# Four layers on one core: S5's direct term folded into its kernels, kernels made in four column strips, z in three matmuls per block, and steps moved by one head

## The chip, the cores and the metric

The kernel runs on one core of a Trainium2 chip. The core has TensorE (PE), whose weight loads are listed apart (PEld), VectorE (DVE), ScalarE (ACT), GpSimd (POOL) and SyncE (SP), which here only issues DMAs. The metric is the time of the whole program on the device, in microseconds (us), as the median of several runs; lower is better. The profiled execution is one run of its own, and its trace starts with the first and ends with the last instruction (the span).

## The reference

A stack of four mixers, each with a residual and a layer norm, on 256 tokens of width 2048 in float32. The first is an SSD mixer (a state space layer in chunks of 128), the second Fox (attention of 16 heads with a forget gate), the third MLA (latent attention), the fourth S5. The change touches S5 above all:

```python
def s5_mixer(h, w_in, lam_re, lam_im, log_step, b_re, b_im, c_re, c_im, d_skip, w_glu, b_glu, w_out):
    u, z = jnp.split(h @ w_in, 2, axis=-1)
    lam = lax.complex(lam_re, lam_im)
    step = jnp.exp(log_step)[:, None]
    lam_bar = jnp.exp(lam * step)
    b_bar = ((lam_bar - 1.0) / lam)[..., None] * lax.complex(b_re, b_im)
    ug = u.reshape(bsz, T, S5_GROUPS, S5_GROUP).astype(jnp.complex64)
    bu = jnp.einsum('gpi,btgi->btgp', b_bar, ug)
    ...
    _, states = lax.associative_scan(_diag_linear_combine, (a_seq, bu), axis=1)
    y = jnp.einsum('gip,btgp->btgi', c, states).real.reshape(bsz, T, S5_WIDTH) + d_skip * u
    y = jax.nn.gelu(y)
    y = y * jax.nn.sigmoid(y @ w_glu + b_glu)
    y = y * jax.nn.silu(z)
    return y @ w_out
```

S5 has 128 groups of 16 channels with 64 complex states each. The term `d_skip * u` is the direct term (D). In the SSD mixer, what the change moves is the product of the scores `cb` with the decay.

## The kernel before

Every large product is written in three passes for accuracy: a float32 operand is split into a rounded part (hi) and a rest (lo), and hi·hi, hi·lo and lo·hi are summed. A weight block of half a megabyte (128x1024) comes in by DMA as `raw`, ACT writes `whi` (line 119), DVE writes `wlo` (line 120), and PE uses both. `mm3` does three matmuls 256 columns wide. `proj_T` (lines 136 to 157) has another form: one 512-wide matmul of whi with hi and lo side by side (line 147), one 256-wide matmul of wlo with hi (line 148), two halves in PSUM, and a DVE reduction (line 157) that adds the halves.

The order of the work is written out by hand. `C.tick()` is called after each half block of a projection (16 or 24 matmuls); `C.defer(n, f)` puts f behind the n-th tick from now, `C.behind(f)` behind the last matmul written. Engines run their own instructions in the order in which the program has them, and wait for each other's data and buffers.

The stages in the trace: SSD to about 712 us, Fox to about 1240, MLA to about 1583, S5 from there to the end.

In SSD, for each group of heads `scores` (line 560 on) multiplies the decay table `arena` by `cbp`, two DVE instructions (line 567); line 569 defers it by three ticks.

S5's kernels do not depend on the tokens. They are made ahead, by the generator `s5_params` (line 947), most of it in the Fox stage: 16 steps on POOL (lines 1093 to 1145), each for 8 groups, with a store of `pn` (`P_d`) as the last instruction. Behind a step stands its `turn` on PE (from line 1062): four transposes to `wp` (1070), and eight small matmuls `kp` (1077) of `pn` with the block pair `bd`. ACT copies `wp`, DVE copies `kp` to `kt` (1079), and DMAs store both (`W_d`, `K_d`). A step's turn is written when the next step is called. Fox calls one step behind each of the three last strips of its v projection (line 699) and one at the start of each head (line 715).

In S5 the width is cut in four strips ft of 512. `u_strip` projects u (three matmuls), transposes it by chunks of four tokens and forms the chunk inputs `vp` (line 1300). A scan over the 64 chunks runs on DVE in three pieces (lines 1207 to 1213), `SCAN_US` = 1.9 us of it per tick, and beside it PE projects z in 16 blocks (`z_tile`, line 1333, by `proj_T`). Then, per strip: `near` (line 1396) applies the kernels within a chunk, `far` (1412) the kernels from the scanned states with `mats` loaded from `P_d`, DVE adds both (`ys`, 1416), `back1` transposes (yp2, 1425), `back2` transposes again (yp3, 1435) and adds D times u on DVE (`yt`, 1441), and `gelu` follows a tick later. A list `held` with the function `outputs` sets after how many ticks a strip's half is taken up. After z comes the glu projection, which needs the gelu's results strip by strip, and the output projection.

## Time and profile before

| | us |
|---|---|
| median of 3 runs | 2019.85 (2015.91 to 2023.44) |
| the profiled execution | 2021.63 |
| its span | 2019.8 |
| mean granted TensorE clock | 0.991 |

The page gives busy time per engine first, then the chain of work that ended last, followed back from the last instruction, and the groups of instructions by line. The prediction below quotes the rows on which it rests. A group's row reads: line, engine, operation, result<-operands with their shapes, count, busy time and mean in ns, then the idle time of the engine ahead of it and what ended most of it. A row of the windows view reads: the stretch and its length, for each engine the busy time and the number of instructions (in the order PE, PEld, DVE, ACT, POOL), the granted clock, the DMA share and GB/s. A row of the timeline reads: start, duration, engine, line, operation and count, and in brackets the idle time before and what ended it.

### The profile page before, as it was taken

The numbers are of one execution on the slowest core, as the hardware profiler recorded it, in microseconds if no ns is written. First come the engines' busy times: TensorE is split into PE (matmuls) and PEld (weight loads), VectorE is DVE, ScalarE is ACT, GpSimd is POOL, SyncE is SP. The second block draws the span as 40 slices with busy tenths as digits, with TensorE's granted clock in tenths as the row PEclk, the third lists the DMA queues.
The fourth block names the chain that finished last, engine by engine and source line by source line (L and its number), as shares of the span: only waits on it lengthen the run. The fifth ranks groups of instructions, "written<-read, shape, count | busy, mean of one in ns | idle before, by whom it ended". The sixth has DMA issues, their size and how long they took to land.

```text
span 2019.8 us, 32021 instructions
## 1 busy us (share of the span) xinstructions
PE 1970.5 (98%) x12169; PEld 1684.2 (83%) x12169; DVE 1470.2 (73%) x2572; ACT 956.4 (47%) x1427; POOL 410.1 (20%) x482
## 2 busy tenths in 40 slices
PE   8999999999999999999999999999999999999997
PEld 6788888888888878788888888988988799878885
DVE  6788788887654596577777567666666778997856
ACT  5455555655433434344444443544654355445442
POOL 0101111011100027999993000000000000110002
PEclk9999999999999999999999999999999999999999
DMA  8555555555665546566566564655357456586552
GB/s 286 185 178 182 183 181 190 178 185 181 206 218 188 185 151 230 179 204 200 199 198 212 173 204 127 207 186 176 126 172 245 175 182 196 169 249 215 193 192 91
DMA packets 116235, 382.42 MB, mean 189 GB/s; under 512 B 18208, under 2 KB 20976, under 8 KB 114288
## 3 DMA queue, kind: packets, MB, share of 16 engines
q1 hardware_dynamic: 103424, 348.11, 52.0%
q0 software_dynamic: 7808, 26.56, 4.2%
q10 hardware_dynamic: 4848, 5.70, 0.8%
q8 instruction: 96, 1.57, 0.3%
q14 instruction: 59, 0.48, 0.1%
HBM read 366.20 MB, written 14.11 MB: 188 GB/s over the span
## 4 chain that ended last, share of the span: by engine, by line
PE 82%; DVE 10%; DMA 3%; POOL 2%; issue 2%; ACT 1%; SPq 0%; DVEq 0%; POOLq 0%; ACTq 0%
PE pT L147 24%; PE pT L148 12%; PE pt L127 10%; PE pt L128 10%; PE pt L126 10%; DVE wlo L120 3%; PE pk L212 2%; PE pk L214 2%; PE pk L213 2%; PE yd L602 1%; DVE hres L339 1%; DVE hres L340 1%; PE o L444 1%; DMA raw<-in_ssd_z 1%; PE kp L1077 1%
## 5 line engine op out<-in xcount | busy, mean ns | idle before, releaser
L120 DVE TENSOR_TENSOR wlo<-raw,whi 128x1024 fp32r<-128x1024 f32 (+4 forms) x612 | 749.5, 1227 | 350.1 <-ACT whi L119 343.7
L119 ACT CAST whi<-raw 128x1024 fp32r<-128x1024 f32 (+4 forms) x612 | 631.3, 1036 | 731.9 <-PE pt L128 320.7
L147 PE MATMUL pT<-h,whi 128*128 128x512 f32 (+2 forms) x2080 | 746.5, 401 | 0.0
L148 PE MATMUL pT<-h,wlo 128*128 128x256 f32 (+2 forms) x2080 | 585.7, 282 | 1.5 <-DVE wlo L120 1.5
L147 PEld LDWEIGHTS pT<-h,whi 128*128 128x128 f32 (+2 forms) x2080 | 389.9, 187 | 94.4 <-issue 0.2
L148 PEld LDWEIGHTS pT<-h,wlo 128*128 128x128 f32 (+2 forms) x2080 | 392.2, 189 | 3.2 <-DVE wlo L120 2.3
L126 PE MATMUL pt<-whi,h 128*128 128x512 f32 (+2 forms) x716 | 281.1, 393 | 6.3 <-ACT whi L119 6.0
L127 PE MATMUL pt<-wlo,h 128*128 128x512 f32 (+2 forms) x716 | 280.0, 391 | 5.8 <-DVE wlo L120 5.6
L128 PE MATMUL pt<-whi,h 128*128 128x512 f32 (+2 forms) x716 | 277.6, 388 | 0.3 <-DVE h L357 0.3
L127 PEld LDWEIGHTS pt<-wlo,h 128*128 128x128 f32 x716 | 136.4, 190 | 35.5 <-DVE wlo L120 8.9
L126 PEld LDWEIGHTS pt<-whi,h 128*128 128x128 f32 x716 | 136.2, 190 | 34.5 <-ACT whi L119 6.4
L128 PEld LDWEIGHTS pt<-whi,h 128*128 128x128 f32 x716 | 136.3, 190 | 26.7 <-issue 1.7
L589 POOL TENSOR_TENSOR xs<-xs,dsk 128x512 f32<-128x512 f32 x16 | 20.8, 1316 | 373.5 <-ACT xs L585 373.5
L126 PE MATMUL pt<-whi,yh 128*128 128x512 f32 x240 | 95.5, 398 | 0.0
L127 PE MATMUL pt<-wlo,yh 128*128 128x512 f32 x240 | 95.4, 397 | 0.0
L128 PE MATMUL pt<-whi,yl 128*128 128x512 f32 x240 | 94.9, 395 | 0.0
L147 PE MATMUL pT<-y,whi 128*128 128x512 f32 x256 | 90.9, 400 | 0.0
L1179 POOL DMA_DIRECT2D mats<-W_d x8 | 4.3, 542 | 336.1 <-DVE h L292 265.7
L148 PE MATMUL pT<-y,wlo 128*128 128x256 f32 x256 | 72.0, 281 | 0.0
L496 DVE SCALAR_TENSOR_TENSOR conv<-u,cw,conv 128x255 f32<-128x255 f32 x144 | 68.8, 479 | 2.2
L89 POOL MEMSET mask<- 128x256 f32 x2 | 0.6, 314 | 302.1 <-PE pt L128 164.4
L147 PEld LDWEIGHTS pT<-y,whi 128*128 128x128 f32 x256 | 48.1, 188 | 12.0 <-DVE y L292 0.2
(469 smaller groups left out, 3050.3 us busy)
## 6 DMA issues: line engine op xcount, KB each, us to landing
raw<-in_ssd_x SPq DMA_DIRECT2D x64, 512.0 KB
raw<-in_ssd_o SPq DMA_DIRECT2D x64, 512.0 KB
raw<-in_ssd_z SPq DMA_DIRECT2D x63, 512.0 KB
raw<-in_fox_v SPq DMA_DIRECT2D x32, 512.0 KB
raw<-in_fox_q SPq DMA_DIRECT2D x32, 512.0 KB
raw<-in_fox_k SPq DMA_DIRECT2D x32, 512.0 KB
raw<-in_fox_z SPq DMA_DIRECT2D x32, 512.0 KB
raw<-in_fox_o SPq DMA_DIRECT2D x32, 512.0 KB
```

What stands on the lines that cost most here:

```text
L119: nc.scalar.copy(hi[:, c], r[:, c])
L120: nc.vector.tensor_tensor(lo[:, c], r[:, c], hi[:, c], op=ALU.subtract)
L126: mm(ps, s[0], m[0], start=first, stop=False)
L127: mm(ps, s[0], m[1], start=False, stop=False)
L128: self.last = mm(ps, s[1], m[0], start=False, stop=last).ins
L147: mm(ps, hi, hT[2][order[kb]], start=kb == 0, stop=False)
L148: self.last = mm(ps[:, 0], lo, hT[0][order[kb]], start=False, stop=kb == KB - 1).ins
L212: mm(o, ws[0], a[0], start=kb == 0 and c % 2 == 0, stop=False)
L213: mm(o, ws[0], a[1], start=False, stop=False)
L214: self.last = mm(o, ws[1], a[0], start=False, stop=end).ins
L496: nc.vector.scalar_tensor_tensor(c[:, k:], u[:, 0:T - k], cw[:, ti, 3 - k:4 - k], c[:, k:], op0=ALU.mult, op1=ALU.add)
L589: nc.gpsimd.tensor_tensor(heads(xs[c]), heads(xs[c]), bc(dsk, g), op=ALU.mult)
```

## The change

It has six parts.

1. In SSD, the first group's `scores` are deferred by six ticks in place of three.
2. In Fox, head 0 calls no step of `s5_params`, so that every later step and turn stands one head later.
3. `kp` is made in four column strips of 32 (positions 0, 32, 64, 96), and the eight matmuls go round the strips; before, they filled two strips, one after the other, each with twice the columns. `kt` has the two halves e on partitions 0 to 63 and 64 to 127.
4. The direct term is put into the kernel of offset 0: `kt`'s columns 48 to 64 are `kp` plus an identity times the skip column of the step. `back2` then needs no product with D, and the gelu reads PSUM on ACT, in the same tick. The table of D in the last layer goes.
5. `z_tile` uses three 256-wide matmuls per block (`proj_T3`), tanh and the product read PSUM, and there is no reduction.
6. `SCAN_US` is 2.2; the `mats` of the last strip go into the buffer of the first scan piece (XA), and the waits in `outputs` change.

```diff
@@ -152,2 +152,11 @@
+    def proj_T3(self, src, hT, ps):
+        for i in range(2):
+            w = self.half(src, i)
+            for j in range(8):
+                kb = 8 * i + j
+                self.mm3(ps, [x[:, j * P:(j + 1) * P] for x in w], [x[kb] for x in hT[0:2]], kb == 0, kb == KB - 1)
+            self.tick()
     def proj_T(self, src, hT, out, m=P, order=range(KB)):
@@ -568,3 +577,3 @@
-            C.defer(3, scores)
+            C.defer(3 if g else 6, scores)
             xp = []
@@ -714,3 +723,4 @@
                 nc.gpsimd.tensor_tensor(ckm, ck, mask, op=ALU.add)
-            C.behind(lambda: next(steps, None))
+            if h:
+                C.behind(lambda: next(steps, None))
             qk = []
@@ -1061,3 +1071,9 @@
     bd = [sq.tile([P, 4, 2, 32], F32, name=f"bd{n}") for n in range(2)]
-    kt = [sq.tile([64, 2, 112], F32, name=f"kt{n}") for n in range(2)]
+    kt = [sq.tile([P, 112], F32, name=f"kt{n}") for n in range(2)]
+    eye, skip = sq.tile([P, 16], F32, name="eye"), sq.tile([P, 16], F32, name="skip")
+    nc.sync.dma_start(skip, A["s5_dk"])
+    V.tensor_tensor(eye, C.ident[:, 0:16], C.ident[:, 16:32], op=Ad)
+    for k0 in range(32, P, 16):
+        V.tensor_tensor(eye, eye, C.ident[:, k0:k0 + 16], op=Ad)
     for t in bd + kt:
@@ -1072,9 +1088,13 @@
         nc.scalar.copy(wt, wp.rearrange("p q b c f -> p (q b c f)"))
         kp = C.aux("kp")
-        for qq in range(2):
+        for c in range(2):
             for e in range(2):
-                for c in range(2):
-                    nc.tensor.matmul(kp[32 * qq:32 * qq + 32, e * 64:(e + 1) * 64], d[:, 2 * qq + e, c],
-                                     pn[:, c, 2 * qq + e, 0:4].rearrange("p r i -> p (r i)"), start=c == 0, stop=c == 1)
-        V.tensor_copy(kt[n % 2][:, :, 48:], kp[0:64, 0:128].rearrange("p (e f) -> p e f", e=2))
+                for qq in range(2):
+                    r0 = 64 * e + 32 * qq
+                    nc.tensor.matmul(kp[r0:r0 + 32, 0:64], d[:, 2 * qq + e, c],
+                                     pn[:, c, 2 * qq + e, 0:4].rearrange("p r i -> p (r i)"), start=c == 0, stop=c == 1,
+                                     tile_position=(0, r0))
+        V.tensor_copy(kt[n % 2][:, 64:], kp[:, 16:64])
+        V.scalar_tensor_tensor(kt[n % 2][:, 48:64], eye, skip[:, n:n + 1], kp[:, 0:16], op0=M, op1=Ad)
         ft, gh = n // 4, n % 4
@@ -1085,3 +1105,3 @@
         for e in range(2):
-            nc.scalar.dma_start(C.K_d[ft, gh // 2, e, :, gh % 2].rearrange("i b f -> b i f"), kt[n % 2][:, e])
+            nc.scalar.dma_start(C.K_d[ft, gh // 2, e, :, gh % 2].rearrange("i b f -> b i f"), kt[n % 2][64 * e:64 * e + 64])
@@ -1163,5 +1183,3 @@
     with C.tc.tile_pool(name="s5", bufs=1) as sp, C.tc.tile_pool(name="s5_w", bufs=1) as wp, C.tc.tile_pool(name="s5_t", bufs=1) as tp:
-        dT = sp.tile([P, KB], F32, name="dT")
         bg = sp.tile([P, KB], F32, name="bg")
-        nc.sync.dma_start(dT, A["s5_dT"])
         nc.sync.dma_start(bg, A["s5_bgT"])
@@ -1333,6 +1351,7 @@
         def z_tile(kb):
-            C.proj_T(A["s5_z"][kb], hT, zs[kb])
+            zps = C.acc("zps")[:, 0:T]
+            C.proj_T3(A["s5_z"][kb], hT, zps)
             th = tp.tile([P, T], F32, tag="th", name="th", bufs=3)
-            nc.scalar.activation(th, zs[kb], AF.Tanh, scale=0.5)
-            nc.vector.scalar_tensor_tensor(zs[kb], th, 1.0, zs[kb], op0=ALU.add, op1=ALU.mult)
+            nc.scalar.activation(th, zps, AF.Tanh, scale=0.5)
+            nc.vector.scalar_tensor_tensor(zs[kb], th, 1.0, zps, op0=ALU.add, op1=ALU.mult)
@@ -1341,3 +1360,3 @@
-        held = []
+        held, rest = [], []
@@ -1346,5 +1365,11 @@
             tm = shifts(ft, h2)
-            pm = mats(C.P_d[ft].rearrange("p h c j f -> p h (c j f)")[:, 2 * h2:2 * h2 + 2]).rearrange(
-                "p (g c q e f) -> p g c q e f", g=2, c=2, q=2, e=2)
-            held.append((k, C.now, tm, pm))
+            src = C.P_d[ft].rearrange("p h c j f -> p h (c j f)")[:, 2 * h2:2 * h2 + 2]
+            if ft < 3:
+                pm = mats(src)
+            else:
+                if h2 == 0:
+                    rest.append(sp.tile([P, 2, 1024], F32, tag="XA", name="mats3"))
+                pm = rest[0][:, h2]
+                nc.gpsimd.dma_start(pm, src)
+            held.append((k, C.now, tm, pm.rearrange("p (g c q e f) -> p g c q e f", g=2, c=2, q=2, e=2)))
@@ -1356,3 +1381,3 @@
             k, since, tm, pm = held[0]
-            wait = 4 if k == 6 else 3 if k < 6 else 1
+            wait = 4 if k == 6 else 5 if k == 7 else 3
             if C.now >= since + wait and (k > 5 or PIECE[k // 2] in done):
@@ -1369,6 +1394,4 @@
                     rest.append(pm)
-                    if held:
-                        held[0] = (7, C.now) + held[0][2:]
-                    else:
-                        C.defer(3, finish)
+                    if not held:
+                        C.defer(1, finish)
             if held:
@@ -1376,4 +1399,2 @@
-        rest = []
         def finish():
@@ -1382,3 +1403,3 @@
             for h2 in range(2):
-                y_far(3, h2, rest[h2])
+                y_far(3, h2, rest[1 + h2])
@@ -1430,3 +1451,3 @@
         def back2(ft, yt):
-            yf = [yt[:, gq // 2].rearrange("p r g i -> p (r g i)")[:, gq % 2 * T:(gq % 2 + 1) * T] for gq in range(4)]
+            y4 = sp.tile([P, 2, 4, T], F32R, tag=f"xu{ft}", name=f"y4{ft}")
             for hq in range(2):
@@ -1435,3 +1456,3 @@
                     tr(yp3[:, r * P:(r + 1) * P], yt[:, hq, r].rearrange("p g i -> p (g i)"), C.ident)
-                src = yp3.rearrange("p (r a c) -> p a r c", r=L, a=2)
+                src = yp3.rearrange("p (r a k m) -> p a r k m", r=L, a=2, k=4)
                 for a in range(2):
@@ -1439,15 +1460,6 @@
                     kb = 4 * gq + ft
-                    dst = yf[gq].rearrange("p (r c) -> p r c", r=L)
-                    nc.vector.scalar_tensor_tensor(dst, uX[ft][:, :, gq], dT[:, kb:kb + 1], src[:, a], op0=ALU.mult, op1=ALU.add)
-            C.defer(1, lambda: gelu(ft, yf))
-        def gelu(ft, yf):
-            y4 = sp.tile([P, 2, 4, T], F32R, tag=f"xu{ft}", name=f"y4{ft}")
-            for gq in range(4):
-                kb = 4 * gq + ft
-                yh[kb], yl[kb], yb[kb] = y4[:, 0, gq], y4[:, 1, gq], y4[:, :, gq]
-                g = tp.tile([P, T], F32, tag="gl", name="gl", bufs=2)
-                nc.scalar.activation(g.rearrange("p (m k r) -> p r k m", k=4, r=L), yf[gq].rearrange("p (r k m) -> p r k m", r=L, k=4),
-                                     AF.Gelu_apprx_tanh)
-                C.split(yh[kb], yl[kb], g)
+                    yh[kb], yl[kb], yb[kb] = y4[:, 0, gq], y4[:, 1, gq], y4[:, :, gq]
+                    g = tp.tile([P, T], F32, tag="gl", name="gl", bufs=2)
+                    nc.scalar.activation(g.rearrange("p (m k r) -> p r k m", k=4, r=L), src[:, a], AF.Gelu_apprx_tanh)
+                    C.split(yh[kb], yl[kb], g)
             ready.append(ft)
@@ -1477,3 +1489,3 @@
-SCAN_US = 1.9
+SCAN_US = 2.2
 LAT_STRIPS = (364, 362, 362)
@@ -1553,3 +1565,3 @@
     o["s5_o"] = k_blocks(g["s5_w_out"][0])
-    o["s5_dT"] = np.ascontiguousarray(g["s5_d"][0].reshape(KB, P).T)
+    o["s5_dk"] = np.ascontiguousarray(g["s5_d"][0].reshape(2, 2, 16, 2, 16).transpose(3, 0, 1, 4, 2).reshape(P, 16))
     o["s5_bgT"] = np.ascontiguousarray(g["s5_b_glu"][0].reshape(KB, P).T)
```

Where it moves instructions, as the two programs have them, engine by engine. PE at the start of Fox's heads, from the end of the v projection (line 128): before, two turns stand there, ahead of head 0's q projection (lines 147 and 148).

```order
L128 MATMUL pt_7235<-whi,h_6497 128x512
L1070 MATMUL wp<-ident,wn 128x2x64 x4
L1077 MATMUL kp<-pn,bd_6979 32x64 x8
L1070 MATMUL wp<-ident,wn 128x2x64 x4
L1077 MATMUL kp<-pn,bd_6978 32x64 x8
L147 MATMUL pT<-h_6344,whi 128x512
L148 MATMUL pT<-h_6344,wlo 128x256
```

After the change (its lines are 1086 for wp and 1095 for kp) one of them stands there:

```order
L128 MATMUL pt_7246<-whi,h_6497 128x512
L1086 MATMUL wp<-ident,wn 128x2x64 x4
L1095 MATMUL kp<-pn,bd_6979 32x64 x8
L147 MATMUL pT<-h_6344,whi 128x512
L148 MATMUL pT<-h_6344,wlo 128x256
L147 MATMUL pT<-h_6344,whi 128x512
```

The other stands 96 projection matmuls later, behind head 0's logits (lps, three rows):

```order
L147 MATMUL pT<-h_6497,whi 128x512
L148 MATMUL pT<-h_6497,wlo 128x256
L736 MATMUL lps<-fox_k,fox_q 128x128
L737 MATMUL lps<-fox_k,fox_q 128x128
L738 MATMUL lps<-fox_k,fox_q 128x128
L1086 MATMUL wp<-ident,wn 128x2x64 x4
L1095 MATMUL kp<-pn,bd_6978 32x64 x8
L147 MATMUL pT<-h_6344,whi 128x512
L148 MATMUL pT<-h_6344,wlo 128x256
```

The second turn has moved behind head 0, and so has each later turn behind its head.

DVE in SSD's first group, from the decay table (16 products) to the wlo that follows; `conv`, `xc` and the reduction of `u` belong to the next strip of the input projection. Before:

```order
L538 SCALAR_TENSOR_TENSOR arena<-arena,tok,upm 128x128 x16
L567 TENSOR_TENSOR arena<-arena,cbp 128x1024 x2
L496 SCALAR_TENSOR_TENSOR conv<-u,cw,conv 128x254
L157 TENSOR_REDUCE u<-pT 128x256
L496 SCALAR_TENSOR_TENSOR conv<-u,cw,conv 128x253
L120 TENSOR_TENSOR wlo<-raw,whi 128x1024
```

After (line 547 for 538, 576 for 567, 505 and 508 for 496 and 499, 166 for 157):

```order
L547 SCALAR_TENSOR_TENSOR arena<-arena,tok,upm 128x128 x16
L505 SCALAR_TENSOR_TENSOR conv<-u,cw,conv 128x254
L576 TENSOR_TENSOR arena<-arena,cbp 128x1024
L505 SCALAR_TENSOR_TENSOR conv<-u,cw,conv 128x253
L576 TENSOR_TENSOR arena<-arena,cbp 128x1024
L508 SCALAR_TENSOR_TENSOR xc<-xc,conv 128x256
L166 TENSOR_REDUCE u<-pT 128x256
L120 TENSOR_TENSOR wlo<-raw,whi 128x1024
```

The two products are spread among the convolution's operations, both still ahead of that wlo, and one xc has come ahead of it.

PE at the end of z, with the last strip's far, yp2 (two groups of transposes) and yp3; lines 147 and 148 are the glu projection here. Before:

```order
L1425 MATMUL yp_18425<-ident,ys 128x128 x2
L1425 MATMUL yp_18431<-ident,ys 128x128 x2
L147 MATMUL pT<-y_17411,whi 128x512
L148 MATMUL pT<-y_17411,wlo 128x256
L147 MATMUL pT<-y_17411,whi 128x512
L1425 MATMUL yp_18425<-ident,ys 128x128 x2
L1425 MATMUL yp_18431<-ident,ys 128x128 x2
L148 MATMUL pT<-y_17411,wlo 128x256
L147 MATMUL pT<-y_17411,whi 128x512
L148 MATMUL pT<-y_17411,wlo 128x256
L1435 MATMUL yp_18437<-ident,yt 128x128 x4
L1435 MATMUL yp_18444<-ident,yt 128x128 x4
```

After, the far is 24 matmuls further back; the last yp2 and its neighbours, and then the last yp3 and the start of glu:

```order
L128 MATMUL zps<-h_15278,wlo 128x256
L1446 MATMUL yp_18643<-ident,ys 128x128 x4
L1446 MATMUL yp_18649<-ident,ys 128x128 x4
L126 MATMUL zps<-h_15398,whi 128x256
L127 MATMUL zps<-h_15398,whi 128x256
L128 MATMUL zps<-h_15398,wlo 128x256
```

```order
L126 MATMUL zps<-h_15418,whi 128x256
L127 MATMUL zps<-h_15418,whi 128x256
L128 MATMUL zps<-h_15418,wlo 128x256
L1456 MATMUL yp_18686<-ident,yt 128x128 x4
L1456 MATMUL yp_18699<-ident,yt 128x128 x4
L147 MATMUL pT<-y_17505,whi 128x512
L148 MATMUL pT<-y_17505,wlo 128x256
L147 MATMUL pT<-y_17505,whi 128x512
```

Before, the last strip's transposes ran into the start of glu; now the last of them stands ahead of it, with 24 matmuls of z between yp2 and yp3.

## The prediction, made before the run

> **What bounds the kernel now.** I read the page first (span, busy shares, chain), then the list of what TensorE waited for, then the windows of the three stages that the change touches.
>
> ```profile
> span 2019.8 us, 32021 instructions
> PE 1970.5 (98%) x12169; PEld 1684.2 (83%) x12169; DVE 1470.2 (73%) x2572; ACT 956.4 (47%) x1427; POOL 410.1 (20%) x482
> ...
> PE 82%; DVE 10%; DMA 3%; POOL 2%; issue 2%; ACT 1%; SPq 0%; DVEq 0%; POOLq 0%; ACTq 0%
> ```
>
> TensorE (PE) is busy 98% of the span and is 82% of the chain that ended last. So time can be saved in two ways only: fewer or denser PE instructions, or fewer of the 49 us (2019.8 - 1970.5) in which PE stands. Work taken from VectorE (DVE, 73%) or ScalarE counts only where PE waits for it. The waits in the last layer's z stage (1699 to 1829 us) are four:
>
> ```profile
> PE far L1412 <- DVE yt L1441: 3.0, 1, 3.0
> PE yp L1425 <- DVE ys L1416: 2.8, 1, 2.8
> PE far L1412 <- DMA mats<-P_d: 2.3, 1, 2.3
> PE pT L148 <- DVE wlo L120: 1.5, 1, 1.5
> ```
>
> The columns are the total in us, how often, and the longest. The windows view agrees, and shows what the stage is made of:
>
> ```profile
> 1699.40:1829.00 129.60, 120.01 (x1481) 104.49 (x1479) 122.64 (x276) 62.27 (x101) 13.26 (x22) 0.99 0.73 216
> ```
>
> Of 129.6 us PE works 120.0; the 9.6 left is the sum of the four waits. DVE works 122.6: here, and only here among the stages touched, a second engine is as full as PE.
>
> **Fox: the S5 steps one head later.** PE's timeline at the start of the heads, first the turn that came too early, then an ordinary one:
>
> ```profile
> 814.90 0.66 PE L1070 MATMUL wp<-ident,wn 128*128 128x128 f32 x4
> 818.34 0.30 PE L1077 MATMUL kp<-pn,bd 128*32 128x64 f32 x2 [2.79 <-POOL pn L1132]
> 820.83 1.28 PE L1077 MATMUL kp<-pn,bd 128*32 128x64 f32 x14 [2.19 <-POOL pn L1139]
> 822.04 0.80 PE L147 MATMUL pT<-h,whi 128*128 128x512 f32 x1
> ```
>
> ```profile
> 842.07 0.60 PE L1070 MATMUL wp<-ident,wn 128*128 128x128 f32 x4
> 842.60 0.89 PE L1077 MATMUL kp<-pn,bd 128*32 128x64 f32 x16
> 843.41 0.50 PE L147 MATMUL pT<-h,whi 128*128 128x512 f32 x1
> ```
>
> From wp to the next projection the early turn takes 822.04 - 814.90 = 7.14 us, the ordinary one 843.41 - 842.07 = 1.34. PE reached step 2's kp before GpSimd (POOL) had its pn. The change moves this turn behind head 0's projections and logits, so 5.80 us goes. A second part follows from the clock (the last three columns of a window are the granted clock, the DMA share and GB/s):
>
> ```profile
> 816.94:820.35 3.41, 0.30 (x2) 0.14 (x2) 0.63 (x1) 0.26 (x1) 3.25 (x4) 1.00 0.68 225
> 822.10:827.10 5.00, 5.00 (x16) 4.25 (x16) 0.28 (x1) 0.00 (x0) 4.51 (x12) 0.50 0.46 130
> 827.20:840.00 12.80, 12.80 (x75) 11.12 (x74) 7.21 (x7) 5.26 (x5) 12.33 (x15) 1.00 0.43 141
> 1786.32:1789.74 3.42, 2.00 (x44) 1.69 (x42) 3.22 (x13) 0.95 (x1) 0.58 (x1) 1.00 0.99 306
> ```
>
> After a stretch with 0.30 us of work in 3.41 the clock was 0.50, and 16 matmuls took 5.00 us; at full clock 75 took 12.80, which is 0.171 each and 2.73 for 16. That is another 2.27. Fox: **-8.1 us**.
>
> Is the wait only put off? POOL's timeline shows when step 2 and the steps behind it are done:
>
> ```profile
> 821.30 0.91 POOL L1145 DMA_DIRECT2D P_d<-pn  x1
> 838.15 0.91 POOL L1145 DMA_DIRECT2D P_d<-pn  x1
> 857.42 0.91 POOL L1145 DMA_DIRECT2D P_d<-pn  x1
> ```
>
> The P_d store is a step's last POOL instruction, and it now comes for steps 2, 3 and 4. The new kp of step 2 stands 96 matmuls later, 814.90 + 96 x 0.171 = 831.3 or a little more, some 10 us after 821.30. Its successors stand where before the next step's kp stood (842.60 for step 3, done at 838.15, and so on), with about 20 us between steps on both engines. What is late next is nothing on PE. On POOL a turn that is later holds the wn buffers (two) and the bd pair longer: step n+2 writes wn after step n's wp. Step 4's wn comes behind step 3's store at 838.15, and wp of step 2 is now through at 832. The mask additions (L714) go ahead of one step more; they take 0.75 us, and POOL is no bound. At the end of the heads the last turn moves from head 12 to head 13 (of 0 to 15), still ahead of anything that reads its result.
>
> **kp in four strips (L1075 to L1079; 1090 to 1100 after).** A turn's kp is 8 matmuls that leave 16 records. They filled two strips of 32 columns, first all of one and then all of the other; now they go round four strips.
>
> ```profile
> L1077 PE MATMUL kp<-pn,bd x256: 219/219/315, 790.4 to 1084.0; 128*32 128x64 f32 x128
> L1079 DVE COPY kt<-kp x16: 272/274/285, 791.4 to 1084.5; 64x128 f32<-64x128 f32 x16
> 1632.06:1633.15 1.09, 1.09 (x64) 1.02 (x64) 1.00 1.03 395
> ```
>
> The last record starts 0.89 - 0.22 = 0.67 us after the first: 15 steps of 45 ns. Line 1300 (third row, four 64x64 tiles in turn) does 64 records in 1.09 us; without the last one's own 0.22, that is 0.87 / 63 = 14 ns. At that pace kp needs 15 x 14 = 0.21 and saves 0.46 in each of 16 turns: **-7.2 us** (16 x 0.45). The bounds are 0, if strips that share all 128 rows don't run side by side more than now, and 16 x 0.67 = -10.7, if kp cost nothing. I take the row of line 1300 as nearest: same passes, same size of output, four tiles. kp's leader (the change of array shape from 128 to 32 columns) and its trailer stay.
>
> Do strips that share their rows overlap at all? Three windows of line 1077 alone, in one turn: the first strip, the crossing from the first to the second, the second.
>
> ```profile
> 842.59:842.84 0.25, 0.24 (x4) 0.25 (x5) 1.00 1.28 410
> 842.84:843.05 0.21, 0.21 (x11) 0.21 (x10) 1.00 0.82 332
> 843.05:843.28 0.23, 0.23 (x12) 0.23 (x6) 1.00 0.91 356
> ```
>
> Weight loads (the second count; matmuls run on from one window into the next) come 5, 10 and 6 to a window: at the crossing, where both strips have work, twice as many. There is a rule against this part. The Trainium skill, "TensorE: Matmul & The Clock Gate", Part 3 (The mechanism), says that weight loads overlap matmuls in flight only where the row group differs; by it kp would stay at 0.67 and the term would be 0. The crossing speaks against that for two strips; no row shows four. The first rival prices it.
>
> The rest of this part lies beside PE. kt's one copy (0.27 us) becomes a copy and a product with the skip (D) column, at most twice that, on DVE, 16 times; seven additions of 128x16 and a small load are new once, and the dT load goes. In Fox, PE's path does not run through DVE (kt is stored two steps later), so this costs 0; without that cover it would be 16 x 0.27 = 4.4 us.
>
> **S5: z in three matmuls, D in the kernels, scan 2.2.** PE first:
>
> ```profile
> 1657.60:1672.09 14.49, 14.49 (x125) 14.49 (x121) 13.87 (x30) 6.53 (x12) 0.53 (x1) 1.00 0.48 150
> 1747.86:1762.15 14.29, 14.29 (x83) 12.16 (x80) 13.89 (x26) 9.12 (x16) 0.00 (x0) 1.00 0.38 125
> ```
>
> The first window is five half blocks of 24 256-wide matmuls of the u projection (120; the window cuts five neighbours), 2.90 us each. The second is five half blocks of z in the present form, a 512-wide and a 256-wide matmul per block of rows (80), 2.86 each. z takes the first form: 32 half blocks x 0.04 = **+1.3 us** on PE.
>
> In return DVE loses work in the z stage (columns: busy us, mean ns, idle before):
>
> ```profile
> L120 DVE TENSOR_TENSOR wlo<-raw,whi 128x1024 fp32r<-128x1024 f32 x34 | 41.4, 1218 | 3.0 <-ACT whi L119 2.9
> L1213 DVE TENSOR_TENSOR X<-X,sc 128x512 f32<-128x512 f32 (+4 forms) x46 | 19.2, 417 | 0.9
> L157 DVE TENSOR_REDUCE zs<-pT 128x256 f32<-128x512 f32 x15 | 10.2, 682 | 0.0
> L1441 DVE SCALAR_TENSOR_TENSOR yt<-xu,dT,yp 128x256 f32<-128x256 f32 x8 | 3.4, 474 | 0.0
> ```
>
> The reduction of z's two halves goes (16 x 0.68 = 10.9 us) and the D product too (16 x 0.47 = 7.6). But the scan, whose four operations per step look like the second row, gets 2.2 us per tick in place of 1.9. Per tick (a half block, 2.9 us of PE) DVE had 1.22 for wlo, 1.9 for the scan and 0.34 for half a reduction, 3.5 in all; now it has 1.22 + 2.2 = 3.4. So while a scan runs DVE stays over PE's pace and lags as now; only the scan is over sooner (by 2.2 / 1.9, a seventh fewer ticks).
>
> Which of the four waits go? "far after yt" (3.0) goes with L1441 itself: back2 now hands PSUM straight to the gelu. "far after DMA" (2.3) goes, since the last two mats get a buffer of their own and no longer wait for near to free one. "yp after ys" (2.8) stays: the two additions still stand between scan steps on DVE, and yp still comes two ticks behind far. It exists at three places (the pieces ft 0, 1, 2) and bites at one now; I count one more, between none and two more (0 to 5.6), because more scan stands ahead of each addition and the row that bit is the only price. The 1.5 stays. S5: -3.0 - 2.3 + 2.8 + 1.3 = **-1.2 us**.
>
> **SSD: the first products three ticks later.** In DVE's order both products of scores and decay still precede the wlo for which PE waits; one xc (below) has come between. PE's wait there (3.3 of the second row) grows by that:
>
> ```profile
> 68.33 4.29 DVE L538 SCALAR_TENSOR_TENSOR arena<-arena,tok,upm 128x128 f32<-128x128 f32 x16 [3.36 <-DMA arena<-acs_d]
> ...
> 77.32 0.42 DVE L499 SCALAR_TENSOR_TENSOR xc<-xc,conv 128x256 f32<-128x256 f32 x1
> ...
> PE pt L127 <- DVE wlo L120: 6.5, 5, 3.3
> ```
>
> At most +0.42, at least 0 (a DMA sets when the products' own chain starts, first row, in both versions): **+0.3 us**.
>
> **Sum.** -8.1 - 7.2 - 1.2 + 0.3 = -16.2 us on the profiled execution, 2021.63 us, gives 2005.4. That execution lies 1.8 us above the median of the three runs (2019.85), so on the median: **2003.6, said as 2003.5**.
>
> **The rivals.**
> - *Strips gain nothing.* The term of -7.2 is 0: 2010.7. For it: kp's strips take all 128 rows, unlike line 1300's tiles. Against: the crossing. Chance 0.10.
> - *S5 lags.* DVE has more scan per tick, yp waits at all three places (+2.8 over the forecast), and each halves the clock for a window as the present one does, 1.7 of 3.4 us lost (below): +2.8 + 3 x 1.7 = +7.9, 2011.4. For it: DVE's 122.6 of 129.6. Against: 18 us less DVE work. Chance 0.12.
>
> ```profile
> 1741.96:1745.36 3.40, 3.30 (x13) 3.04 (x14) 3.33 (x5) 1.17 (x2) 0.00 (x0) 0.50 0.66 244
> ```
>
> - *S5 catches up.* DVE's saving is enough: all waits of the stage go, -9.6, and one half clock (-1.7), +1.3: -10.0 in place of -1.2, so 1994.7. For it: those 18 us are more than all four waits. Against: they fall mostly outside the scan's ticks. Chance 0.10.
> - *The Fox wait only moves*, to a later kp or to POOL's buffers: 2003.5 + 8.1 = 2011.6. Against it stand the P_d rows with 10 us and more to spare. Chance 0.04.
> - *Slower: each change of strip costs a drain.* kp now changes strip 7 times a turn and not once. The nearest price is the step from kp's last start (843.27) to the next projection (843.41), 0.14 us where the array's shape changes. 16 x 7 x 0.14 = +15.7 in place of -7.2: 2026.4. It makes the whole change slower from 9.0 / 112 = 0.08 us per change. Against: line 1300 changes tile at every record and takes 14 ns for it. Chance 0.04.
>
> **Numbers.** The forecast has 0.60. The range leaves out the slow tail and little of the fast one: 1995 to 2012 takes in the rivals at 2010.7, 2011.4, 2011.6 and, just, 1994.7, with the bounds of kp (-3.5 more) and of yp (-2.8 and +2.8). About 0.5%, 10.1 us, is what a measurement of this kernel can tell from no change, so "faster" is under 2009.75. The forecast and "S5 catches up" make 0.70, the near edges of the rivals that end at 2010.7 to 2011.6 another 0.05: faster 0.75, same 0.21, slower 0.04.
>
> **What would show it.** In the new profile: no PE wait on pn near 815 to 835 and full clock there; kp's 16 records from first to last start in about 0.2 us and the next projection about 0.45 us sooner after kp's first; z's half blocks at 2.90; no wait of far on DVE or mats; at most two waits of yp. The prediction is wrong if kp's records still spread over 0.67 us, if the waits of yp come with clock 0.50 three times, or if some later kp waits for pn.

## The result, and the profile after

| | before | after |
|---|---|---|
| median of the runs beside each other, us | 2019.18 (4 runs) | 1997.44 (4 runs, 1996.08 to 1998.54) |
| ratio, 95% interval | | 0.9898 (0.988 to 0.9917) |
| profiled execution, us | 2021.63 | 1996.87 |

The forecast was 2003.5 (1995 to 2012). The gain on the medians is 21.7 us where 16.3 was forecast. The page of the profile after, its lines for the span, the engines and the chain:

```profile
span 1995.1 us, 32537 instructions
PE 1956.7 (98%) x12425; PEld 1685.5 (84%) x12425; DVE 1462.7 (73%) x2563; ACT 953.9 (48%) x1427; POOL 411.1 (21%) x482
...
PE 86%; DVE 10%; DMA 2%; issue 2%; ACT 1%; SPq 0%; DVEq 0%; ACTq 0%; POOLq 0%
```

PE is still the bound, with a larger share of the chain; POOL has left it. Cutting both traces at the same PE instructions (the first matmul, the first transposes behind SSD, the first latent transposes of MLA, the first transposes behind MLA, the last matmul) says where the 24.8 us between the two profiled executions lie:

| stretch | before | after | difference | forecast |
|---|---|---|---|---|
| up to the first matmul | 5.63 | 5.26 | -0.4 | 0 |
| SSD | 703.55 | 699.55 | -4.0 | +0.3 |
| Fox, with the layer boundary | 586.33 | 567.98 | -18.4 | -15.3 |
| MLA | 286.19 | 284.99 | -1.2 | 0 |
| S5, to the last matmul | 424.59 | 423.80 | -0.8 | -1.2 |

In Fox, PE's timeline after the change of the turn that is now step 2's, and of an ordinary one:

```profile
827.42 0.60 PE L1086 MATMUL wp<-ident,wn 128*128 128x128 f32 x4
827.95 0.43 PE L1095 MATMUL kp<-pn,bd 128*32 128x64 f32 x16
828.31 0.50 PE L147 MATMUL pT<-h,whi 128*128 128x512 f32 x1
...
846.82 0.60 PE L1086 MATMUL wp<-ident,wn 128*128 128x128 f32 x4
847.35 0.43 PE L1095 MATMUL kp<-pn,bd 128*32 128x64 f32 x16
847.71 0.50 PE L147 MATMUL pT<-h,whi 128*128 128x512 f32 x1
```

Neither waits. The turn is 0.89 us long (847.71 - 846.82), the old one was 1.34; kp's records last 0.43 in all where they lasted 0.89. Step 2's turn came at 827.4, forecast at 831 or more, and POOL was far ahead: its store of step 2's pn starts at 819.3.

In z, the list of PE's waits from 1670 to 1810 us:

```profile
PE yp L1446 <- DVE ys L1437: 4.4, 2, 2.4
PE yp L1446 <- DVE sc L1229: 1.0, 1, 1.0
```

Both waits of far are gone and the one at wlo too; yp waits at all three places, 5.4 us together. A window of three half blocks of z, and two pairs of windows around yp's longer waits:

```profile
1698.71:1707.53 8.82, 8.82 (x78) 8.69 (x72) 8.44 (x24) 2.38 (x3) 1.26 (x3) 1.00 0.88 240
1715.48:1718.89 3.41, 1.06 (x10) 0.85 (x9) 3.41 (x7) 1.35 (x2) 0.00 (x0) 1.00 1.04 222
1718.90:1722.30 3.40, 3.40 (x18) 3.40 (x18) 3.30 (x6) 1.05 (x3) 0.00 (x0) 0.50 0.96 374
1773.50:1776.91 3.41, 1.33 (x12) 1.12 (x11) 3.41 (x7) 1.60 (x3) 0.00 (x0) 1.00 0.99 317
1776.92:1780.33 3.41, 3.41 (x18) 3.41 (x17) 1.44 (x2) 0.80 (x3) 0.00 (x0) 0.50 0.94 336
```

A half block of z takes 8.82 / 3 = 2.94 us, not 2.90, and two of the waits halved the clock where one had.

MLA's -1.2 is a wait ahead of its end that only the profile before has. Its list of PE's waits from 1296 to 1580 us is one line:

```profile
PE pt L127 <- DVE wlo L120: 1.1, 1, 1.1
```

### The profile page after: what moved, and what is told of

It reads as the page before. It is cut to its first block, busy times and chain, and to the rows that moved or that the text cites. A ratio compares the mean times of both kernels' runs of the same rounds, so it can differ in the third digit from the quotient of the medians.

```text
span 1995.1 us, 32537 instructions
## 1 busy us (share of the span) xinstructions
PE 1956.7 (98%) x12425; PEld 1685.5 (84%) x12425; DVE 1462.7 (73%) x2563; ACT 953.9 (48%) x1427; POOL 411.1 (21%) x482
## 4 chain that ended last, share of the span: by engine, by line
PE 86%; DVE 10%; DMA 2%; issue 2%; ACT 1%; SPq 0%; DVEq 0%; ACTq 0%; POOLq 0%
PE pT L147 23%; PE pT L148 12%; PE pt L127 12%; PE pt L126 12%; PE pt L128 12%; DVE wlo L120 2%; PE pk L221 2%; PE pk L222 2%; PE pk L223 2%; PE yd L611 1%; DVE hres L348 1%; DVE hres L349 1%; PE zps L126 1%; DMA raw<-in_ssd_z 1%; PE o L453 1%
## 5 line engine op out<-in xcount | busy, mean ns | idle before, releaser
L147 PE MATMUL pT<-h,whi 128*128 128x512 f32 (+1 forms) x1824 | 648.7, 399 | 0.0
L148 PE MATMUL pT<-h,wlo 128*128 128x256 f32 (+1 forms) x1824 | 511.1, 280 | 0.0
L147 PEld LDWEIGHTS pT<-h,whi 128*128 128x128 f32 (+1 forms) x1824 | 340.0, 186 | 81.2
L148 PEld LDWEIGHTS pT<-h,wlo 128*128 128x128 f32 (+1 forms) x1824 | 341.8, 187 | 1.0
L126 PE MATMUL zps<-h,whi 128*128 128x256 f32 x256 | 75.7, 296 | 0.0
L127 PE MATMUL zps<-h,whi 128*128 128x256 f32 x256 | 73.8, 288 | 0.0
L128 PE MATMUL zps<-h,wlo 128*128 128x256 f32 x256 | 73.7, 288 | 0.0
```

The lines of the kernel that those rows point to most:

```text
L126: mm(ps, s[0], m[0], start=first, stop=False)
L127: mm(ps, s[0], m[1], start=False, stop=False)
L128: self.last = mm(ps, s[1], m[0], start=False, stop=last).ins
L147: mm(ps, hi, hT[2][order[kb]], start=kb == 0, stop=False)
L148: self.last = mm(ps[:, 0], lo, hT[0][order[kb]], start=False, stop=kb == KB - 1).ins
```

## The experiments

Times are medians; the ratios are to the kernel before on the same chip.

### The step alone, and the strips alone

The kernel before with one of the two Fox edits:

```diff
-            C.behind(lambda: next(steps, None))
+            if h:
+                C.behind(lambda: next(steps, None))
```

> The kernel before with head 0 calling no step, nothing else. Theory: the turn of 7.14 us at 814.9 becomes one of 1.35 and the stretch of 0.50 clock behind it goes, together -8.1 us in Fox; no later kp waits for pn; from head to head the distance of the turns stays 20.06 us. Rival (the pace of the projections comes with the moved steps): the distance falls to 19.86, which is another 2.8 us over 14 heads.

Measured: 2011.02 us against 2018.09, ratio 0.9963 (0.9949 to 0.9977), which is 4.6 to 10.3 us less; forecast -8.1. Fox with its layer boundary is 577.7 us long, 6.7 to 8.6 less than in the two profiles without either Fox edit (584.4 in the SSD kernel below, 586.3 before). No kp waits, and the distance of the turns stays 20.06. From the turn ahead of head 0 to the turn behind it PE takes 19.1 us where it took 28.5; step 2's turn itself, 1.34, now stands behind head 0, so 8.1 us went. The theory holds.

```diff
-                    nc.tensor.matmul(kp[32 * qq:32 * qq + 32, e * 64:(e + 1) * 64], ...
+                    nc.tensor.matmul(kp[r0:r0 + 32, 0:64], ..., tile_position=(0, r0))
-        V.tensor_copy(kt[n % 2][:, :, 48:], kp[0:64, 0:128].rearrange("p (e f) -> p e f", e=2))
+        V.tensor_copy(kt[n % 2][:, 48:], kp[:, 0:64])
```

The order of the loops, the tile kt and its store change with it, as in the whole change.

> The kernel before with kp in four strips and kt on 128 partitions, with D still added on DVE in the last layer. Theory: kp goes from 0.67 to 0.21 us from first to last start in all 16 turns, -7.3 us, and the wait at 818 to 821 (5.0 us) stays; the distance of the turns falls from 20.06 to 19.60, by the kp alone. Rival (the faster pace of the projections, 1.9% in two of three stretches of a head, comes with the strips): the distance falls to 19.40, -10 us in all.

Measured: 2011.67, ratio 0.9969 (0.9956 to 0.9982), which is 3.6 to 8.9 us less. PE's timeline of two early turns of this kernel:

```profile
812.76 0.43 PE L1078 MATMUL kp<-pn,bd 128*32 128x64 f32 x16
...
814.11 0.55 PE L1070 MATMUL wp<-ident,wn 128*128 128x128 f32 x3 [0.66 <-POOL wn L1139]
816.61 0.32 PE L1078 MATMUL kp<-pn,bd 128*32 128x64 f32 x8 [1.95 <-POOL pn L1134]
819.10 0.44 PE L1078 MATMUL kp<-pn,bd 128*32 128x64 f32 x8 [2.17 <-POOL pn L1141]
```

From first to last start kp takes 0.21 us (0.43 less the last one's own 0.22). The early turn still waits, 4.8 us. The distance of the turns is 19.60, the kp alone: the theory holds, and the faster pace below does not come with the strips.

### Strip by strip

The changed kernel with another order of kp's matmuls:

```diff
-        for c in range(2):
-            for e in range(2):
-                for qq in range(2):
+        for e in range(2):
+            for qq in range(2):
+                for c in range(2):
```

> The changed kernel with kp's eight matmuls in the order strip by strip (two matmuls of a strip behind each other) instead of round the four strips. Theory (a strip's passes wait for each other, and PE runs some three records ahead, as at the crossing of the kernel before): kp takes 0.3 to 0.45 us from first to last start instead of 0.21, some 2 to 4 us in 16 turns. Rival A (only the number of strips counts): 0.21, no change. Rival B (only one strip is at work at a time): 0.67 to 0.8, +7 us or more.

Measured: 2000.51, ratio 0.9911 (0.989 to 0.9931). One turn in PE's timeline:

```profile
847.94 0.60 PE L1086 MATMUL wp<-ident,wn 128*128 128x128 f32 x4
848.47 0.45 PE L1095 MATMUL kp<-pn,bd 128*32 128x64 f32 x16
848.85 0.50 PE L147 MATMUL pT<-h,whi 128*128 128x512 f32 x1
```

kp takes 0.45 in all, 0.02 us longer: rival A, the order hardly counts. So the gain does not come from the distance between the two matmuls that add to the same place either; here they stand behind each other, as before the change. Yet from turn to turn it is 19.62 us and not 19.41. That is 0.21 us a turn for 0.02 us of kp. The rest is in the projections, which the next part takes up.

### Where the faster pace of Fox's projections comes from

After the change a turn comes every 19.41 us, where the kp accounts for 19.60. The last 24 pairs of matmuls (a 512-wide and a 256-wide one, `proj_T`) ahead of the logits, in the windows view, before and after:

```profile
913.06:921.62 8.56, 8.56 (x51) 7.43 (x50) 5.85 (x6) 3.07 (x4) 8.15 (x11) 1.00 0.70 230
```

```profile
915.37:923.78 8.41, 8.41 (x51) 7.37 (x50) 6.02 (x6) 3.07 (x4) 8.00 (x12) 1.00 0.68 214
```

The same matmuls at the same clock take 8.56 and 8.41 us, 353 against 347 ns a pair away from the ends. No stretch of Fox's heads has a pace between. Two kernels ask what sets it. The first is the kernel before with the three parts outside S5:

> The kernel before with the three parts outside the last layer (scores deferred by six, steps one head later, kp in four strips) and the last layer as before, D on DVE. Theory (the last layer's parts bring next to nothing, as the stage's own length in the two profiles has it, 424.6 against 423.8 us): the time is within 2 us of the changed kernel's 1997.4. Rival (the medians of the strips alone and the step alone leave some 7 us, which the last layer must have brought): 2003 to 2005. For the pace of Fox's projections: a distance of turns of 19.41 if strips and step together set it, 19.60 if the second DVE operation on kp (the D product) does.

Measured: 2003.84, ratio 0.9926 (0.9909 to 0.9942), 6.4 us above the changed kernel's median; the turns are 19.60 us apart, so strips and step together do not set the pace. S5 takes 424.0 us in this profile, 0.2 more than after the change. The profiled execution, at 2000.78, is the fastest of this kernel's four; the stages of its trace bear out the theory on S5, the median stands with the rival. The second is the changed kernel without the direct term:

```diff
-        V.tensor_copy(kt[n % 2][:, 64:], kp[:, 16:64])
-        V.scalar_tensor_tensor(kt[n % 2][:, 48:64], eye, skip[:, n:n + 1], kp[:, 0:16], op0=M, op1=Ad)
+        V.tensor_copy(kt[n % 2][:, 48:], kp[:, 0:64])
```

> The changed kernel with kt made by one copy, as before, so that it leaves out the direct term; the identity and the skip column are still made, nothing else differs. It asks where the faster pace of Fox's projections comes from, which the kernel with strips and step but without D does not have (19.60 us from turn to turn). Theory (the second DVE operation on kp, which lets kp's PSUM bank go later): the distance is 19.60 again. Rival (what is made ahead of the steps: the seven additions, the load, the two tiles and the addresses behind them): it stays at 19.41.

Measured: one run, 1996.68, turns 19.41 apart. The theory falls: the second operation on kp is not it. What sets the pace stays open. The kernel with the scores at three ticks (below) has distances of 19.50, 19.51 and 19.31 in turn, with the same instructions in Fox as the changed kernel; each stretch of 8, 16 or 24 pairs keeps the pace in which it begins. So a stretch falls into one of two rhythms, and a small shift of its start (0.02 us of kp in the kernel above) seems to suffice. MLA, whose code no edit touches, has the same two: its stretch of 224 pairs runs at 353 ns a pair in eight of the 14 profiles, those of before and after among them, and at 347 in six. In Fox all seven profiles of changed kernels that keep the order of kp and the scores at six ticks have 19.41. No run shows what the start is measured against, nor whether the kernel's code or the execution decides in Fox.

### SSD's scores

The kernel before with that edit alone, and the changed kernel without it:

```diff
-            C.defer(3, scores)
+            C.defer(3 if g else 6, scores)
```

> The kernel before with the first group's scores deferred by six ticks, nothing else. Theory (the deferral itself pays): PE has the decay-free work ahead of its need for the products, the 3.3 us wait on wlo near 77 us shrinks to about 1 us, the stretch of 0.50 clock behind it goes, and everything behind it is 4 us earlier: the first transpose of the layer boundary (PE, ptr) at 705 +- 0.5 us instead of 709.2. Rival (the order on DVE alone, as the prediction had it): the wait is 3.3 to 3.7 us, the 0.50 clock stays, and ptr comes at 709.2 to 709.6; what the changed kernel gained there would be the acs_d transfer that landed 1.2 us earlier in its profiled run.

> The changed kernel with the first group's scores deferred by three ticks again. Theory (the deferral pays): the wait on wlo of about 3 us and the 0.50 clock near 77 us come back, the first ptr moves from 704.8 to 709 +- 0.5, and the time rises by about 4 us. Rival: ptr stays at 704.8 to 705.3, no change in time.

Measured: with it alone 2017.14, ratio 0.9999 (0.9988 to 1.001); the changed kernel without it 1997.93 against 1997.44. The first transposes behind SSD come at 706.5 in the one, which is neither the theory's 705 nor the rival's 709.2, and at 708.3 in the other, near the theory's 709; but the time does not rise by the 4 us that the theory had. The lists of PE's waits from 60 to 100 us, with the edit alone, then after the change, then the changed kernel without the edit:

```profile
PE xp L576 <- DVE xc L499: 3.0, 1, 3.0
```

```profile
PE xp L585 <- DVE xc L508: 1.2, 1, 1.2
```

```profile
PE pt L127 <- DVE wlo L120: 3.3, 1, 3.3
```

The edit turns a wait on wlo into one on xc, which the prediction did not see. How long it is hangs on the transfer of `acs_d`, for which the products of the decay table wait on DVE. Their rows with the edit alone and after the change:

```profile
68.78 4.30 DVE L538 SCALAR_TENSOR_TENSOR arena<-arena,tok,upm 128x128 f32<-128x128 f32 x16 [3.99 <-DMA arena<-acs_d]
```

```profile
67.09 4.29 DVE L547 SCALAR_TENSOR_TENSOR arena<-arena,tok,upm 128x128 f32<-128x128 f32 x16 [2.19 <-DMA arena<-acs_d]
```

From issue to landing the transfer took 9.2 us in the one and 7.4 in the other. Over the 14 profiles PE's wait is this time less 6.2 us in the ten kernels with the edit (6.3 to 9.3 us, waits of 0 to 3.1) and less 5.8 in the four without (9.0 to 9.4, waits of 3.2 to 3.6). So the edit shortens the wait by 0.4 us, and the rival has it right that the transfer, which landed sooner in the profile after, made the rest. Kernels with the same instructions in SSD had 6.3 and 9.3 us; what makes it land sooner is not shown. SSD is 701.3 us long on average in the four profiles with three ticks (698.9 to 703.6), 699.5 in the ten with six (697.8 to 701.2) and 700.3 in the five of these with transfers of 8.8 us or more.

### Which gap halves the clock

In each of the profiles, the stretches of 0.50 clock begin on one grid of 3.413 us that runs through the whole execution, and the grid lies elsewhere in each of them. A grid window is the stretch between two of its lines. The gap at 77 us (about 3.2 us) in the kernel with the step alone falls across a line of the grid:

```profile
72.04:75.45 3.41, 1.58 (x9) 1.02 (x7) 3.41 (x5) 1.66 (x3) 0.00 (x0) 1.00 0.00 0
75.46:78.86 3.40, 2.04 (x10) 1.69 (x11) 3.40 (x7) 2.32 (x4) 0.00 (x0) 1.00 0.27 77
```

Two grid windows with 1.83 and 1.36 us idle, and the clock stays 1.00. In the kernel before, the same gap put 2.1 us into one window (72.83 to 76.24: 1.32 of 3.41 busy) and cost two windows of half clock; with 5.61 us of work in them that is some 2.8 us. Over 14 profiles every window at full clock with up to 1.84 us idle was followed by full clock and every one with 1.94 or more by half; between them there is one of each. A window that is itself at half clock needs less: of ten with 0.42 to 1.60 us idle, nine were followed by a second one at half clock, and none with up to 0.25 us. With 1.92 us idle, full clock (the kernel with three parts); with 1.88, half (the one with the later yp2, below):

```profile
1719.25:1722.66 3.41, 1.49 (x11) 1.44 (x12) 3.38 (x6) 1.82 (x3) 0.00 (x0) 1.00 0.89 302
1722.67:1726.07 3.40, 3.40 (x24) 3.06 (x23) 3.37 (x6) 0.04 (x2) 0.00 (x0) 1.00 0.28 105
```

```profile
1563.32:1566.73 3.41, 1.53 (x8) 1.00 (x9) 3.30 (x10) 0.74 (x2) 0.00 (x0) 1.00 0.00 0
1566.74:1570.14 3.40, 3.40 (x13) 2.90 (x12) 2.90 (x6) 2.38 (x4) 0.00 (x0) 0.50 0.41 77
```

So a gap of 2.0 to 3.6 us costs 1.7 us more, or some 3, or nothing, by where it falls. SSD's -4.0 and S5's -0.8 in the table hold such luck: before, the gap at 77 us and the one at 1592, where S5 begins, each cost two windows. After the change the first is only 1.2 us long and costs none, and the second costs one.

### The last layer

Three edits of the changed kernel, and the third of them with a second one:

```diff
-            zps = C.acc("zps")[:, 0:T]
-            C.proj_T3(A["s5_z"][kb], hT, zps)
+            zps = zs[kb]
+            C.proj_T(A["s5_z"][kb], hT, zps)
```

> The changed kernel with z in its old form, a 512-wide and a 256-wide matmul per block of rows and a reduction on DVE. Theory (in this stage DVE's work sets the waits of yp): PE's z matmuls are 2 to 3 us shorter, DVE has 9.6 us more, the waits of yp grow from 5.4 us by more than 3, and the time is 0 to 4 us higher. Rival (PE's content decides): the waits of yp stay near 5.4 and the time is 2 to 3 us lower.

Measured: 1994.93, ratio 0.9881 (0.9866 to 0.9896). PE's waits in z:

```profile
PE yp L1446 <- DVE ys L1437: 4.5, 2, 3.3
PE far L1433 <- issue: 1.8, 1, 1.8
```

The waits are 6.3 us, 0.9 more than after the change, and S5 takes 421.9 us, 1.9 less. The rival holds: 10.3 us more work on DVE (busy 1473.0 us against 1462.7) cost PE little, and z's three matmuls cost what PE spends on them. The intervals of the two ratios overlap, so the 2.5 us between the medians is not shown by the times alone.

```diff
-SCAN_US = 2.2
+SCAN_US = 1.9
```

> The changed kernel with 1.9 us of scan per tick instead of 2.2. Theory (what is late at yp is the pair of additions queued behind scan steps on DVE): the three waits of yp, 5.4 us, fall to under 2.5, and the time by 1 to 4 us, unless the last piece is done so late that PE waits behind z. Rival (DVE is full either way, the scan only lasts longer): waits of 4 us or more at yp or far, and a time from the same to 5 us higher.

Measured: 1996.87, ratio 0.9887 (0.9872 to 0.9902).

```profile
PE yp L1446 <- DVE sc L1227: 3.2, 1, 3.2
PE yp L1446 <- DVE ys L1437: 2.8, 2, 2.5
PE yp L1446 <- issue: 1.2, 1, 1.2
```

7.2 us of waits in place of 5.4, and the same time, with none of the three gaps followed by half clock in this profile: the theory falls. A slower scan does not bring the additions sooner.

```diff
-                C.defer(2 if ft < 3 else 1, lambda: back1(ft, ys[ft]))
+                C.defer(3 if ft < 3 else 1, lambda: back1(ft, ys[ft]))
```

> The changed kernel with yp2 three ticks behind far instead of two, for the first three strips. Theory (the additions come 8 us after far, a tick of 2.95 us too late, and DVE has slack by the end of z): the waits of yp (5.4 us) and the two stretches of 0.50 clock behind them (some 3 us) go, and no other wait takes their place; 6 to 8 us less time than the changed kernel. Rival (PE's waits are what lets DVE catch up): waits of about 5 us show at wlo in z or at the later yp, and the time is within 2 us of the changed kernel's.

Measured: 1993.55, ratio 0.9868 (0.9853 to 0.9882), the fastest of all.

```profile
PE far L1433 <- issue: 2.4, 1, 2.4
PE yp L1446 <- DVE ys L1437: 0.2, 1, 0.2
```

yp's waits are gone, and one of 2.4 us at a far has come, which starts at 1725.8 as a scan step on DVE ends. S5 takes 418.8 us, 5.0 less than after the change, where four profiles of the changed kernel's S5 agree within 0.3 us; one window of z has 0.50 clock, not two. The medians differ by 3.9, with intervals that just touch, and the profiled execution, at 1988.53, is 5 us under this kernel's median. The theory holds for yp's waits; that no other wait would come, and the size of 6 to 8 us, do not hold. Then the same with 2.5 us of scan per tick, and the same with z in its old form:

> The kernel with yp2 three ticks behind far, and 2.5 us of scan per tick instead of 2.2. Theory (its one wait left in z, 2.4 us at a far that starts as the scan step on DVE ends, comes from a scan a little too late): the far waits less than 0.5 us and the time is 1 to 4 us under that kernel's 1993.6. Rival (DVE is full while the scan runs, so what the scan gains the additions lose): waits of 2 us or more at yp, and a time from the same to 4 us higher.

> The changed kernel with the two edits that paid, z in its old two-matmul form and yp2 three ticks behind far. Theory (they add up: z's form was worth 2.5 us, the later yp2 3.9): 1991 +- 2 us. Rival (the reduction's 9.6 us of DVE time fill the tick that the later yp2 gives): the waits of yp are back at 2 us or more, 1993.5 to 1996.

Measured: 1998.97, ratio 0.9907 (0.9892 to 0.9922), and 1998.03, ratio 0.9893 (0.9876 to 0.991). Both theories fall: S5 takes 424.3 us in both profiles, and what the later yp2 had brought is gone. PE's waits in z, more scan first:

```profile
PE far L1433 <- issue: 6.1, 2, 5.8
PE yp L1446 <- DVE ys L1437: 1.0, 1, 1.0
```

```profile
PE yp L1456 <- ACT yt L1448: 4.5, 2, 2.6
PE pT L148 <- DVE wlo L120: 1.3, 2, 0.8
PE far L1433 <- issue: 0.6, 1, 0.6
PE yp L1446 <- DVE ys L1437: 0.5, 1, 0.5
```

With more scan, far waits 5.8 us instead of 2.4; it starts at 1727.88, 0.1 us after the piece's last step ends on DVE (1727.10 and 0.68 long). With z's old form the wait passes to yp3. ACT's timeline ahead of it:

```profile
1724.50 0.42 ACT L1355 ACTIVATE th<-zs 128x256 f32<-128x256 f32 x1 [6.38 <-DVE zs L166]
1724.82 1.03 ACT L119 CAST whi<-raw 128x1024 fp32r<-128x1024 f32 x1
1725.76 1.06 ACT L1448 COPY yt<-yp 128x512 f32<-128x512 f32 x2
```

ACT's tanh waits 6.4 us for the reduction of z, which is queued between scan steps on DVE, and the copy of yt is queued behind the tanh. So with the later yp2 the new form of z has a use that its own sum does not show: the tanh reads PSUM and needs nothing of DVE, and ACT keeps to time. With yp2 two ticks behind far the old form was no slower, as its own run above showed.

## Why the prediction was right, and where it was off

**Fox's wait, -8.1: right.** The wait of 2.79 + 2.19, the longer turn and the half clock behind it went, nothing later waited for pn, and the step alone measures 4.6 to 10.3 us and 8.1 in PE's timeline. The rival that the wait only moves is out.

**kp in four strips, -7.2: right to a tenth.** The forecast 0.67 to 0.21 us is what 16 turns show. Strips that share all 128 rows do run side by side, so the rule of the Trainium skill ("TensorE: Matmul & The Clock Gate", Part 3) that was quoted against this part gives the wrong result here. The drain rival is out as well: seven changes of strip a turn cost nothing that shows.

**The sum for Fox missed some 2.7 us**, the second rhythm of the projections (14 turns of 0.19). The profile of before has both rhythms, 347 ns a pair in most stretches of SSD and 353 in Fox's heads and in MLA, but nothing in it says which one a changed Fox falls into. The cause is open: the strip order undoes it, and no part of the change was shown to bring it.

**S5, -1.2: the size holds by luck, for two of its terms did not.** Both waits of far went as forecast, and yp waits 5.4 us in all where 2.8 + 2.8 was taken, at three places and not two. The wait of 1.5 at wlo, forecast to stay, went. z's half block is 2.94 and not 2.90, so the term of +1.3 was +2.6 us (32 x 0.08). These two misses cancel. yp halved the clock in two windows, one more than before, and the start of S5 in one, one less. The stage's length fell by 0.8 between the two profiles. Averaged over profiles it fell by 0.4: five with the old S5 (422.5 to 425.6), four with the new (423.6 to 423.8). No run takes the direct term in the kernels, or the own buffer of the last mats, by itself; that they took away the two waits of far is read from the lists alone.

**SSD, +0.3: wrong in its account, small in effect.** The step read DVE's order alone and had the wait on wlo grow. In fact cb's matmuls move on PE, too (from 58.8 to 68.0 us), and PE then waits for xc and not for wlo, 0.4 us less with the same landing of the transfer. The edit alone measures no change.

**The total, -16.3 against -21.7.** Of the 5.4 us on the medians 2.7 is the rhythm, and the rest is within the interval of the measurement (0.988 to 0.9917 is 16.8 to 24.2 us). Between the two profiled executions the sum missed 8.6 us: 4.3 in SSD, where the transfer landed sooner and two windows of half clock fell away, 3.1 in Fox, 1.2 in MLA and 0.4 ahead of the first matmul, less 0.4 in S5. In the profile of before eight grid windows ahead of the end have 0.50, in that of after four; the three kernels with the early turn have six to eight, the eleven without it two to five.

## What to carry to other kernels

Small matmuls that fill different column strips run side by side even where they share all rows: putting eight of them round four strips cut a turn from 1.34 to 0.89 us. When a producer of another engine is late once, at the start, move the consumer behind the next block of work and check the producer's own stores for the margin; here that was worth 7 us between the medians. Where a consumer waits for an engine with a long queue, moving the consumer back (one tick at yp2, 3.9 us between medians, 5.0 in the stage of the profiles) did what a thinner queue (less scan per tick) did not. The gain is easily lost again: more scan per tick, or z's reduction back in ACT's chain, each undid it, though the reduction cost nothing while yp2 stood one tick sooner.

## What the runs showed of the hardware

In these traces the clock is set window by window on a fixed grid of 3.413 us: 57% idle in one window at full clock (1.94 of 3.41 us) halved the next, 54% (1.84) did not, and a gap of 3.2 us that straddled a line cost nothing. A window at half clock was followed by another with as little as 0.42 us idle. So two executions of one program can differ by some us by the place of the grid alone; this is worked out from profiles of different kernels, for none was profiled twice. The Trainium skill ("TensorE: Matmul & The Clock Gate", Part 1) has a window of 3413 ns that runs freely, which these traces bear out, and a halving after an idle window, which they correct: a window 57% idle is enough.

One small transfer (`acs_d` to `arena`) took 6.3 to 9.4 us from issue to landing over the 14 profiles, and PE's wait behind it grew with it, microsecond for microsecond, above 6.2 us (5.8 with the scores at three ticks). A stretch of alternating 512- and 256-wide matmuls runs at 353 or at 347 ns a pair, from its start to its end; 0.02 us of other work ahead of it went with a change from one to the other, and the cause is open.
